# Transposes one at a time between wide products, all four of a copied tile rounded

## The chip, the cores and the metric

The kernel runs on one core of a Trainium2 chip. The metric is the device time of one execution in microseconds, median of several runs. TensorE (PE in the profile; its weight loads are PEld) multiplies, VectorE is DVE, ScalarE is ACT, GpSimd is POOL, SyncE is SP.

## The reference

A decoder trunk of 256 tokens by 2048: a latent attention layer (MLA), an MLP, a Mamba-2 layer (SSM), and a second MLP, each behind an RMS norm and added to the residual stream. All is float32.

```python
def reference(x, ...):
    for i in range(DEPTH):                       # DEPTH = 2
        h = rms_norm(x, mix_norm_g[i])
        mix = mla_mixer(h, ...) if i % 2 == 0 else ssm_mixer(h, ...)
        x = x + mix
        h = rms_norm(x, mlp_norm_g[i])
        x = x + squared_relu_mlp(h, mlp_w_in[i], mlp_w_out[i])
    return x

def squared_relu_mlp(h, w_in, w_out):            # w_in 2048 x 8192, w_out 8192 x 2048
    u = jax.nn.relu(h @ w_in)
    return (u * u) @ w_out
```

## The kernel before, in words

Every large product is done in three rounded-fp32 products (fp32r). A float32 operand is split into a high half (rounded, `wh` of a weight, `h` of an activation) and a low half (the rest, `wl`, `lo`), and high x high, low x high and high x low are added up in PSUM. The weights stream from memory once; ACT makes each high half (line 102) and VectorE each low half (line 103). A wide product has 512 columns of weights moving and a 128x128 block of activations as the stationary operand that a weight load puts in. It is issued from `block` (lines 339, 340 and 343; MLA, SSM and the end of an MLP) or from `products` in `mlp_body` (lines 616 to 618).

The stationary side must have the model dimension on the partitions, so each new activation tile of 128 tokens by 512 columns is transposed on TensorE in four 128x128 pieces into one PSUM bank (pool `sm` or `yp`) by `transposed`; ACT then copies the bank out as the high half (`split_out`, line 299) and VectorE makes the low half (line 300). For the hidden tiles of the MLP, the boundary tiles (`finalize`) and the gated tiles of the SSM layer, `words` first copies the tile with a DMA from POOL's queue into a tile of type fp32r (named `tr`), and a transpose of such a copy runs as rounded fp32 (line 322); the others run as plain fp32 (line 324). `words` takes the number of 128-column pieces that it copies. `by_words` names the hidden tiles of pairs 1 to 6 in the MLP.

TensorE's order is the order of the program's text; the orders of the other engines are set by a scheduler. Work that shall come a little later is put in a queue with `later(n, fn)` and comes out n calls of `tick` later, between two blocks. In the MLP a table of tokens made by a planner sets the order; a clock `at` counts the time that the planner gives to each token (1.36 or 2.72 us), and `turn` and `when` put transposes and other steps at due times on that clock. `combinations` makes sums of activation tiles for the seven-product scheme of the MLP; its steps `one` and `two` are due at 5 and 10 on that clock, and what they make is called `sN5`, `sN6`, `sN7`.

Whatever puts out a transposed tile, the four transposes stand in a row in TensorE's order, and where the two token tiles come in one tick, eight do. The transposes of the attention heads (`s1`, `s3`) and of the convolution (`conv`) are written out by themselves and are no part of this.

Of the kernel before, what the change touches and what calls it, by code (L numbers as in the profile page):

```python
# [28 lines left out]
P = 128  # L29
# [29 lines left out]
class Unit:  # L59
# [3 lines left out]
    def __init__(self, key, nk, n, loads, make):  # L63
        self.key, self.nk, self.n, self.loads, self.make = key, nk, n, loads, make
# [150 lines left out]
class Trunk:  # L215
    def __init__(self, tc, ctx, d, out):
        self.tc, self.nc, self.d, self.out = tc, tc.nc, d, out
        nc = self.nc
        pool = lambda name, bufs, **kw: ctx.enter_context(tc.tile_pool(name=name, bufs=bufs, **kw))
        self.c = pool("const", 1)  # L220
        self.st = pool("stat", 24)
        self.res = pool("res", 1)
        self.xtp = pool("xt", 8)
        self.k4 = pool("k4", 8)
        self.s2 = pool("s2", 7)
        self.gb = pool("gb", 2)
        self.wp = {"raw": pool("raw", 6), "wh": pool("wh", 4), "wl": pool("wl", 4)}
        self.acc = pool("acc", 4, space=PSUM)
        self.sm = pool("sm", 2, space=PSUM)
        self.yp = pool("yp", 2, space=PSUM)  # L230
        self.queue, self.pump = [], None
        self.nsm = 0
        self.uid = 0

# [19 lines left out]
    def drain(self):  # L254
        while self.queue:
            self.tick()

    def stat(self, n):
        return self.st.tile([P, 16], F32, tag="st", name=self.name("st"))[:, :n]
# [54 lines left out]
        self.transposed(src, h[:, :, sl], lo[:, :, sl], wide)  # L314

    def transposed(self, src, h, lo, wide=True):
        b = self.bank(wide)
        src, words, n = src if isinstance(src, tuple) else (src, None, 0)
        for j in range(4):
            v = slice(j * P, (j + 1) * P)  # L320
            if j < n:
                self.nc.tensor.transpose(b.bitcast(F32R)[:, v], words[:, v], self.ident_r)  # L322
            else:
                self.nc.tensor.transpose(b[:, v], src[:, v], self.ident)  # L324
        self.split_out(h, lo, b.rearrange("p (k n) -> p k n", k=4))


    def block(self, keys, lhs, n=512, accs=None, first=True, last=True, mid=None):
        nc = self.nc
        if accs is None:  # L330
            accs = [self.acc_tile() for _ in range(2)]
        kt = 0
        for ik, key in enumerate(keys):
            for nk, wh, wl, end in self.flow.piece(key):
                en = last and ik == len(keys) - 1 and end
                for q in range(nk):
                    for t in range(2):
                        ah, al = lhs(kt + q, t)
                        nc.tensor.matmul(accs[t][:, :n], ah, wh[:, q, :], start=first and kt + q == 0, stop=False)  # L339
                        nc.tensor.matmul(accs[t][:, :n], al, wh[:, q, :], start=False, stop=False)  # L340
                for q in range(nk):
                    for t in range(2):
                        nc.tensor.matmul(accs[t][:, :n], lhs(kt + q, t)[0], wl[:, q, :], start=False, stop=en and q == nk - 1)  # L343
                kt += nk
                if mid and not end:
                    mid()
            self.tick()
        return accs
# [44 lines left out]
    def finalize(self, nb, accs, wide=True):  # L393
        nc = self.nc
        g = self.gain_tile(self.nx_gain[nb])
        if not self.by_tile:
            self.nx[nb] = (self.ktile(self.xtp), self.ktile(self.xtp))
        elif nb % 2 == 0:
            for t in range(2):
                self.nx[nb // 2, t] = [self.ktile(self.xtp).rearrange("p a b -> p (a b)").rearrange("p (k n) -> p k n", n=P)  # L400
                                       for _ in range(2)]
        for t in range(2):
            if self.by_tile:
                h, lo = (v[:, 4 * (nb % 2):4 * (nb % 2) + 4] for v in self.nx[nb // 2, t])
            else:
                h, lo = (v[:, :, t * P:(t + 1) * P] for v in self.nx[nb])
            x = self.x[t][nb]
            nc.vector.tensor_tensor(x, accs[t], x, ALU.add)
            xg = self.scratch()
            nc.vector.tensor_tensor(xg, x, g, ALU.mult)  # L410
            self.square_sum(x, self.nx_ssq[:, t * 4 + nb:t * 4 + nb + 1])
            early = nb < 3 - self.by_tile
            if early:
                xg = self.words(xg, 4 - t)
            self.later(int(early), lambda h=h, lo=lo, xg=xg: self.transposed(xg, h, lo, wide))

    def boundary_end(self):
# [141 lines left out]
    def mlp_body(self, mp, layer, gain):  # L559
# [4 lines left out]
        def hidden(r, pp, j, t):  # L564

            nc.scalar.activation(r, r, AF.Square)
            if (pp, j) not in us:
                us[pp, j] = (self.ktile(self.k4), self.ktile(self.k4))
            h, lo = us[pp, j]
            if by_words(pp, j, t):  # L570
                r = self.words(r, 3, mp)
            return lambda wide: self.transposes(r, h, lo, t, wide)

        def relu(src, t):
# [10 lines left out]
        S, steps = self.combinations(mp, xa)  # L585
        S["M1"], S["N4"], S["M2"] = xa[0, 0], xa[1, 1], xa[1, 0]
        out, bank, v, count = {}, {}, {}, {}
# [3 lines left out]
        def when(us, fn):  # L591
            due.append((at[0] + us, fn))
# [16 lines left out]
        def products(accs, key, lhs, kt, first, last):  # L609
            u, (h, lo) = self.flow.next(key)  # L610
            for q in range(2):
                k = 2 * kt + q
                wh, wl = h[:, q * 512:(q + 1) * 512], lo[:, q * 512:(q + 1) * 512]
                for t, b in enumerate(accs):
                    ah, al = lhs(k, t)
                    nc.tensor.matmul(b, ah, wh, start=first and q == 0, stop=False)  # L616
                    nc.tensor.matmul(b, ah, wl, start=False, stop=False)  # L617
                    nc.tensor.matmul(b, al, wh, start=False, stop=last and q == 1)  # L618

        sub = lambda o, a, b: nc.vector.tensor_tensor(o, a, b, ALU.subtract)  # L620
        plus = lambda o, a, b: nc.vector.tensor_tensor(o, a, b, ALU.add)
# [29 lines left out]

        tokens = plan()
        inside = False
        when(5, steps[0])
        when(10, steps[1])
        for tok in tokens:
            key = (tok[0], layer) + tok[1:]
            if tok[0] == "s":
                _, p, name, d = tok
# [3 lines left out]
                if count.setdefault(name, 0) % 4 == 0:  # L663
                    pool = self.sm if name == "N7" else self.acc
                    bank[name] = pool.tile([P, 512], F32, tag=pool.name, name=self.name("st"))
                count[name] += 1
                products([bank[name]], key, lambda k, t: [x[:, k] for x in S[name]], d,
                         count[name] % 4 == 1, count[name] % 4 == 0)
                if count[name] % 4 == 0:
                    after(name, p)  # L670
                move(1.36)
            elif tok[0] == "c":
                _, p, j, o = tok
# [11 lines left out]
            else:  # L685
                _, p, nb, o = tok
# [380 lines left out]
    def ssm_body(self, sp, dp, gain):  # L1067
# [12 lines left out]
        xg = [None] * GROUPS  # L1080
# [248 lines left out]
        def z_block(g):  # L1329
            accs = self.block([("si", "z", g, q) for q in range(4)], xT)  # L1330
            ng = self.gain_tile(d["sng"][g])
            ssq = self.stat(2)
            ws = []
            for t in range(2):
                w = self.scratch()
                nc.scalar.activation(w, accs[t], AF.Tanh, scale=rsh[t])
                nc.vector.scalar_tensor_tensor(w, w, 1.0, accs[t], ALU.add, ALU.mult)
                ws.append(w)
            yT[g] = (self.ktile(self.k4), self.ktile(self.k4))

            def gate():
                if g not in ready:
                    self.later(0, gate)
                    return
                for t in range(2):
                    x = xg[g][t]
                    nc.gpsimd.tensor_tensor(x, ws[t], x, ALU.mult)
                    self.square_sum(x, ssq[:, t:t + 1], scale=rs[t])
                rr = self.rsqrt(ssq, 2, 512, 4 * EPS)
                r = self.stat(2)  # L1350
                nc.vector.tensor_tensor(r, rr, rs2, ALU.mult)
                for t in range(2):
                    nc.vector.scalar_tensor_tensor(ws[t], xg[g][t], r[:, t:t + 1], ng, ALU.mult, ALU.mult)
                    w = self.words(ws[t], 4 - t)
                    self.later(2, lambda t=t, w=w: self.transposes(w, yT[g][0], yT[g][1], t, False))
                self.later(2, lambda: gated.add(g))

            self.later(0, gate)
# [50 lines left out]
def by_words(p, j, t):  # L1409

    return 0 < p < 7
# [196 lines left out]
```

## Time and profile before

| what | value |
|---|---|
| runs | 2288.2, 2285.67, 2287.46 us; median 2287.46 us |
| profiled execution, span from first to last instruction | 2284.5 us |
| TensorE busy | 2278.1 us, 10929 products |
| VectorE, ScalarE, GpSimd busy | 84%, 61%, 12% of the span |
| TensorE clock granted | 1.000 over the span |
| rounded transposes of `transposed` (line 322) | 249 |
| plain transposes of `transposed` (line 324) | 183 |

The profile gives the span of the profiled execution, and for its own time nothing beyond it; the runs are 1.2 to 3.7 us longer than that span. Products overlap in TensorE's pipeline, so the sum of their recorded durations says little; the distance from one start to the next says what each costs. In a timeline, neighbouring instructions of one line and shape are merged into one row with a count.

### The profile page before, as it was taken

How to read it: one execution, taken by the hardware profiler on the slowest of the kernel's cores; microseconds unless marked ns; L12 is line 12 of the kernel's file. 1: busy time of each engine (PE TensorE's matmuls, PEld its weight loads, DVE VectorE, ACT ScalarE, POOL GpSimd, SP SyncE). 2: the span in 40 equal slices, each digit the busy share in tenths (PEclk: the TensorE clock that was granted, in tenths of full speed). 3: DMA queues.
4: the chain of work that ended last, by engine and by line, in shares of the span. 5: the costliest groups of instructions: out<-in, count | busy, mean ns of one | idle time of the engine just before them, and what ended most of it. 6: DMA issues, size and time to landing. Idle time of an engine off the chain costs nothing.

```text
span 2284.5 us, 30768 instructions
## 1 busy us (share of the span) xinstructions
PE 2278.1 (100%) x10929; PEld 1889.6 (83%) x10929; DVE 1915.9 (84%) x2318; ACT 1390.1 (61%) x1947; POOL 275.5 (12%) x315
## 2 busy tenths in 40 slices
PE   9999999999999999999999999999999999999999
PEld 7898888888888888888888888888888888888887
DVE  7786698999898897687899688676989889989985
ACT  7775576566666666564666555545666666666663
POOL 1440000000000000100133213121000000000000
PEclk9999999999999999999999999999999999999999
DMA  8545678888888878667888787767688888888874
GB/s 315 173 153 159 211 230 267 259 255 270 264 255 259 267 232 271 227 208 241 277 280 278 245 275 264 229 222 229 204 265 248 259 270 253 260 275 247 267 232 160
DMA packets 167706, 557.16 MB, mean 244 GB/s; under 512 B 19040, under 2 KB 28192, under 8 KB 166528
## 3 DMA queue, kind: packets, MB, share of 16 engines
q1 hardware_dynamic: 151264, 502.44, 66.2%
q0 software_dynamic: 13888, 48.49, 10.0%
q10 hardware_dynamic: 2400, 4.27, 0.5%
q8 instruction: 86, 1.41, 0.3%
q14 instruction: 68, 0.56, 0.1%
HBM read 529.65 MB, written 6.41 MB: 235 GB/s over the span
## 4 chain that ended last, share of the span: by engine, by line
PE 96%; DVE 1%; DMA 1%; ACT 1%; issue 1%; POOL 0%; SPq 0%; ACTq 0%; DVEq 0%
PE acc L339 13%; PE acc L340 13%; PE acc L343 13%; PE yp L618 9%; PE yp L617 9%; PE yp L616 9%; PE st L617 7%; PE st L618 7%; PE st L616 7%; DMA wraw<-mi 1%; PE sm L324 1%; DVE wl L103 1%; PE y L1309 1%; PE sm L322 1%; PE acc L616 1%; PE acc L618 1%
## 5 line engine op out<-in xcount | busy, mean ns | idle before, releaser
L102 ACT ACTIVATE wh<-wraw 128x1024 fp32r<-128x1024 f32 (+1 forms) x818 | 856.2, 1053 | 570.4 <-PE acc L340 268.9
L103 DVE TENSOR_TENSOR wl<-wraw,wh 128x1024 fp32r<-128x1024 f32 (+1 forms) x818 | 985.5, 1221 | 240.6 <-ACT wh L102 216.6
L616 PE MATMUL yp<-wh,k 128*128 128x512 f32 x896 | 349.2, 390 | 0.0
L618 PE MATMUL yp<-wh,k 128*128 128x512 f32 x896 | 348.8, 389 | 0.0
L617 PE MATMUL yp<-wl,k 128*128 128x512 f32 x896 | 348.6, 389 | 0.0
L339 PE MATMUL acc<-wh,xt 128*128 128x512 f32 x704 | 279.7, 397 | 0.4 <-ACT wh L102 0.4
L340 PE MATMUL acc<-wh,xt 128*128 128x512 f32 x704 | 274.9, 390 | 0.1
L102 ACT ACTIVATE wh<-wrx 128x1024 fp32r<-128x1024 f32 x168 | 177.8, 1058 | 153.4 <-PE yp L618 101.7
L103 DVE TENSOR_TENSOR wl<-wrx,wh 128x1024 fp32r<-128x1024 f32 x168 | 204.3, 1221 | 36.6 <-ACT wh L102 35.6
L618 PEld LDWEIGHTS yp<-wh,k 128*128 128x128 f32 x896 | 168.2, 188 | 35.1
L617 PEld LDWEIGHTS yp<-wl,k 128*128 128x128 f32 x896 | 168.2, 188 | 34.9
L616 PEld LDWEIGHTS yp<-wh,k 128*128 128x128 f32 x896 | 168.2, 188 | 34.8
L339 PE MATMUL acc<-wh,k 128*128 128x512 f32 x496 | 196.5, 396 | 0.0
L340 PE MATMUL acc<-wh,k 128*128 128x512 f32 x496 | 193.3, 390 | 0.0
L343 PE MATMUL acc<-wl,xt 128*128 128x512 f32 x704 | 188.3, 389 | 0.0
L616 PE MATMUL st<-wh,xt 128*128 128x512 f32 x448 | 177.7, 397 | 0.0
L618 PE MATMUL st<-wh,xt 128*128 128x512 f32 x448 | 174.9, 390 | 0.0
L617 PE MATMUL st<-wl,xt 128*128 128x512 f32 x448 | 174.7, 390 | 0.0
L339 PEld LDWEIGHTS acc<-wh,xt 128*128 128x128 f32 x704 | 132.7, 188 | 29.4 <-ACT wh L102 1.6
L340 PEld LDWEIGHTS acc<-wh,xt 128*128 128x128 f32 x704 | 132.5, 188 | 28.5 <-issue 1.2
L343 PEld LDWEIGHTS acc<-wl,xt 128*128 128x128 f32 x704 | 132.1, 188 | 27.7
L199 POOL DMA_DIRECT2D wrx<-mi x56 | 49.2, 878 | 720.6 <-DVE wl L103 524.5
(318 smaller groups left out, 3527.0 us busy)
## 6 DMA issues: line engine op xcount, KB each, us to landing
wraw<-mi SPq DMA_DIRECT2D x256, 512.0 KB, 5.5
wraw<-mo SPq DMA_DIRECT2D x256, 512.0 KB, 5.6
wraw<-si SPq DMA_DIRECT2D x160, 512.0 KB, 5.2
wraw<-so SPq DMA_DIRECT2D x64, 512.0 KB, 5.2
wrx<-mi SPq DMA_DIRECT2D x56, 512.0 KB, 5.4
wrx<-mi POOLq DMA_DIRECT2D x56, 512.0 KB, 7.8
wraw<-wo SPq DMA_DIRECT2D x32, 512.0 KB, 4.0
taps<-xD SPq DMA_DIRECT2D x16, 768.0 KB, 8.4
```

What stands on the lines that cost most here:

```text
L102: self.last = nc.scalar.activation(h[:, v], raw[:, v], AF.Copy)
L103: self.last_lo = nc.vector.tensor_tensor(lo[:, v], raw[:, v], h[:, v].bitcast(F32), ALU.subtract)
L199: nc.gpsimd.dma_start(st["b11"].tile, quarter(d, 1, 0), accum_op=ALU.add)
L322: self.nc.tensor.transpose(b.bitcast(F32R)[:, v], words[:, v], self.ident_r)
L324: self.nc.tensor.transpose(b[:, v], src[:, v], self.ident)
L339: nc.tensor.matmul(accs[t][:, :n], ah, wh[:, q, :], start=first and kt + q == 0, stop=False)
L340: nc.tensor.matmul(accs[t][:, :n], al, wh[:, q, :], start=False, stop=False)
L343: nc.tensor.matmul(accs[t][:, :n], lhs(kt + q, t)[0], wl[:, q, :], start=False, stop=en and q == nk - 1)
L616: nc.tensor.matmul(b, ah, wh, start=first and q == 0, stop=False)
L617: nc.tensor.matmul(b, ah, wl, start=False, stop=False)
L618: nc.tensor.matmul(b, al, wh, start=False, stop=last and q == 1)
L1309: nc.tensor.matmul(y[t][c, o], part(t)[:, c], xg[g][t][:, o], start=True, stop=True)
```

## The change

`transposed` no longer issues its four transposes. It puts four closures in a list `drops`, and `drip`, called behind every wide product of `block` and of `products`, issues one of them. The bank is taken with the first of the four, and the copy out of it follows the fourth. `drain` flushes what is left at the end. Where word copies are made, all four pieces of a tile are copied now and all four transposes run rounded; before it was three in the MLP's hidden tiles and in the tile of the second 128 tokens elsewhere. The two steps of the combinations are due at 8 and 12.

```diff
         self.queue, self.pump = [], None
+        self.drops = []
...
     def drain(self):
         while self.queue:
             self.tick()
+        self.flush()
+
+    def drip(self):
+        if self.drops:
+            self.drops.pop(0)()
+
+    def flush(self):
+        while self.drops:
+            self.drip()
...
     def transposed(self, src, h, lo, wide=True):
-        b = self.bank(wide)
         src, words, n = src if isinstance(src, tuple) else (src, None, 0)
-        for j in range(4):
-            v = slice(j * P, (j + 1) * P)
+        bank = []
+
+        def one(j):
+            if not bank:
+                bank.append(self.bank(wide))
+            b, v = bank[0], slice(j * P, (j + 1) * P)
             if j < n:
                 self.nc.tensor.transpose(b.bitcast(F32R)[:, v], words[:, v], self.ident_r)
             else:
                 self.nc.tensor.transpose(b[:, v], src[:, v], self.ident)
-        self.split_out(h, lo, b.rearrange("p (k n) -> p k n", k=4))
+            if j == 3:
+                self.split_out(h, lo, b.rearrange("p (k n) -> p k n", k=4))
+
+        for j in range(4):
+            self.drops.append(lambda j=j: one(j))
...
     def block(...):
                         nc.tensor.matmul(accs[t][:, :n], ah, wh[:, q, :], start=first and kt + q == 0, stop=False)
+                        self.drip()
                         nc.tensor.matmul(accs[t][:, :n], al, wh[:, q, :], start=False, stop=False)
+                        self.drip()
...
                         nc.tensor.matmul(accs[t][:, :n], lhs(kt + q, t)[0], wl[:, q, :], start=False, stop=en and q == nk - 1)
+                        self.drip()
...
     def finalize(...):
-                xg = self.words(xg, 4 - t)
+                xg = self.words(xg, 4)
...
     def hidden(...):
-                r = self.words(r, 3, mp)
+                r = self.words(r, 4, mp)
...
     def products(...):
                     nc.tensor.matmul(b, ah, wh, start=first and q == 0, stop=False)
+                    self.drip()
                     nc.tensor.matmul(b, ah, wl, start=False, stop=False)
+                    self.drip()
                     nc.tensor.matmul(b, al, wh, start=False, stop=last and q == 1)
+                    self.drip()
...
-        when(5, steps[0])
-        when(10, steps[1])
+        when(8, steps[0])
+        when(12, steps[1])
...
     def gate():
-                    w = self.words(ws[t], 4 - t)
+                    w = self.words(ws[t], 4)
```

On TensorE, in the first MLP, a hidden tile (`k`) of pair 0 is the operand of wide products while another hidden tile, copied as `tr`, is transposed into a bank of `sm`. Before:

```order
L618 MATMUL yp_3896<-wh_3866,k_433_3271 128x512
L322 MATMUL sm_3933<-ident,tr_3785 128x128 x3
L324 MATMUL sm_3933<-ident,s_457_3776 128x128
L616 MATMUL yp_3895<-wh_3878,k_445_3557 128x512
L617 MATMUL yp_3895<-wl_3879,k_445_3557 128x512
```

The three rounded transposes and the plain one stand in a row. The same place on TensorE after the change (line 335 is a rounded transpose there, 636, 638 and 640 are the wide products of `products`):

```order
L636 MATMUL yp_3895<-wh_3878,k_445_3557 128x512
L335 MATMUL sm_3940<-ident,tr_3785 128x128
L638 MATMUL yp_3895<-wl_3879,k_445_3557 128x512
L335 MATMUL sm_3940<-ident,tr_3785 128x128
L640 MATMUL yp_3895<-wh_3878,k_446_3558 128x512
L335 MATMUL sm_3940<-ident,tr_3785 128x128
L636 MATMUL yp_3896<-wh_3878,k_445_3557 128x512
L335 MATMUL sm_3940<-ident,tr_3785 128x128
L638 MATMUL yp_3896<-wl_3879,k_445_3557 128x512
```

Each transpose has a wide product on either side, the fourth is rounded too, and the row's end lies three wide products further on.

On TensorE, in the MLA stage, the two token tiles of the key and value latent (`ckv`) are transposed behind the query products of head pair 1 (384 columns) and then used. Before, eight plain transposes and the end of the query products:

```order
L324 MATMUL sm_782<-ident,s_57_706 128x128 x4
L324 MATMUL sm_789<-ident,s_58_708 128x128 x4
L339 MATMUL yp_762<-wh_728,cq_199 128x384
L340 MATMUL yp_762<-wh_728,cq_200 128x384
L339 MATMUL yp_763<-wh_728,cq_199 128x384
L340 MATMUL yp_763<-wh_728,cq_200 128x384
```

Twelve query products stood between the last transpose and the first product that reads `ckv`. After (337 is a plain transpose, 356, 358 and 362 the products of `block`):

```order
L356 MATMUL yp_763<-wh_728,cq_199 128x384
L337 MATMUL sm_800<-ident,s_58_708 128x128
L358 MATMUL yp_763<-wh_728,cq_200 128x384
L337 MATMUL sm_800<-ident,s_58_708 128x128
L362 MATMUL yp_762<-wl_729,cq_199 128x384
L362 MATMUL yp_763<-wl_729,cq_199 128x384
L362 MATMUL yp_762<-wl_729,cq_199 128x384
L362 MATMUL yp_763<-wl_729,cq_199 128x384
L356 MATMUL acc_864<-wh_746,ckv_201 128x512
L358 MATMUL acc_864<-wh_746,ckv_202 128x512
```

Four query products are left between the last transpose and the first use. On ScalarE, which waits for those transposes, before:

```order
L102 ACTIVATE wh_798<-wraw_726 128x768
L299 ACTIVATE ckv_201<-sm_782 128x4x128
L299 ACTIVATE ckv_201<-sm_789 128x4x128
L102 ACTIVATE wh_868<-wraw_744 128x768
L296 ACTIVATE s_83_828,st_827<-yp_762 128x192
```

And after, at the same place on ScalarE:

```order
L102 ACTIVATE wh_784<-wraw_726 128x768
L309 ACTIVATE ckv_201<-sm_789 128x4x128
L102 ACTIVATE wh_868<-wraw_744 128x768
L309 ACTIVATE ckv_201<-sm_800 128x4x128
L306 ACTIVATE s_83_828,st_827<-yp_762 128x192
```

A weight conversion (line 102) now stands between the two copies out of the banks.

## The prediction, made before the changed kernel was run

> **What bounds the kernel.** I read the page's busy shares and chain first, then the waits of TensorE, then the timeline around single transposes. The page:
>
> ```profile
> span 2284.5 us, 30768 instructions
> PE 2278.1 (100%) x10929; PEld 1889.6 (83%) x10929; DVE 1915.9 (84%) x2318; ACT 1390.1 (61%) x1947; POOL 275.5 (12%) x315
> PE 96%; DVE 1%; DMA 1%; ACT 1%; issue 1%; POOL 0%; SPq 0%; ACTq 0%; DVEq 0%
> ```
>
> The busy line, then the chain by engine. TensorE never stops, and the chain is TensorE to 96%. The waits of the weight loads say the same; this is the largest:
>
> ```profile
> PEld st L617 <- DVE wl L103: 3.2, 8, 0.5
> ```
>
> So 3.2 us in eight waits, of 2284. Whatever TensorE issues is paid in full: a shorter or longer place in its stream moves the end by as much, and work of the other engines counts only where it would make TensorE wait. The measure of everything is the step from one wide product to the next:
>
> ```profile
> 500.38 0.39 PE L616 MATMUL yp<-wh,k 128*128 128x512 f32 x1
> ...
> 511.26 0.39 PE L616 MATMUL st<-wh,sN 128*128 128x512 f32 x1
> ```
>
> There are 48 steps between these two, so 10.88/48 = 0.2267 us each. The recorded 0.39 is longer than the step because products overlap in the pipeline; starts are what counts.
>
> The transposes that the change touches, by shape (L322 are the rounded ones, that read a word copy; L324 the plain fp32 ones):
>
> ```profile
> L324 PE MATMUL sm<-ident,s 128*128 128x128 f32 x167 | 33.7, 281 | 0.0
> L322 PE MATMUL sm<-ident,tr 128*128 128x128 f32 x229 | 26.9, 236 | 0.0
> L324 PE MATMUL yp<-ident,s 128*128 128x128 f32 x16 | 2.4, 272 | 0.0
> L322 PE MATMUL yp<-ident,tr 128*128 128x128 f32 x20 | 2.3, 236 | 0.0
> ```
>
> 249 rounded and 183 plain, 432 in all. In the program's order they stand in 86 rows: 48 rows of three rounded and one plain, 15 of seven rounded and one plain, 16 of four plain, 7 of eight plain.
>
> **What the rows cost now.** The price of a row is the time from the last wide product before it to the second one behind it, less two steps (the second, because the first one's record starts early and is long). Three rounded and one plain:
>
> ```profile
> 374.36 0.39 PE L617 MATMUL yp<-wl,k 128*128 128x512 f32 x1
> 374.59 0.39 PE L618 MATMUL yp<-wh,k 128*128 128x512 f32 x1
> 374.82 0.37 PE L322 MATMUL sm<-ident,tr 128*128 128x128 f32 x3
> 375.02 0.30 PE L324 MATMUL sm<-ident,s 128*128 128x128 f32 x1
> ...
> 375.39 0.40 PE L617 MATMUL yp<-wl,k 128*128 128x512 f32 x1
> ...
> 377.71 0.39 PE L618 MATMUL yp<-wh,k 128*128 128x512 f32 x1
> ```
>
> 375.39 - 374.59 - 2 x 0.2267 = 0.347 us. (To 377.71 there are ten more steps, in 2.32 us and not 2.27: a tail of about 0.04 us in which wide products run a little slow, whose cause I don't know.) Seven rounded and one plain, then four plain, then eight plain:
>
> ```profile
> 231.46 0.85 PE L343 MATMUL acc<-wl,k 128*128 128x512 f32 x3
> 232.14 0.46 PE L322 MATMUL yp<-ident,tr 128*128 128x128 f32 x4
> ...
> 233.05 0.39 PE L340 MATMUL acc<-wh,k 128*128 128x512 f32 x1
> ```
>
> ```profile
> 297.85 0.39 PE L618 MATMUL yp<-wh,xt 128*128 128x512 f32 x1
> 298.08 0.60 PE L324 MATMUL sm<-ident,s 128*128 128x128 f32 x4
> ...
> 298.75 0.40 PE L617 MATMUL yp<-wl,xt 128*128 128x512 f32 x1
> ```
>
> ```profile
> 277.79 0.39 PE L618 MATMUL acc<-wh,xt 128*128 128x512 f32 x1
> 278.02 0.60 PE L324 MATMUL yp<-ident,s 128*128 128x128 f32 x4
> ...
> 279.12 0.40 PE L617 MATMUL acc<-wl,xt 128*128 128x512 f32 x1
> ```
>
> 1.59 - 4 x 0.2267 = 0.683 us (three wide products stand in the first line), 0.90 - 0.453 = 0.447 us and 1.33 - 0.453 = 0.877 us. From the pairs: one more rounded transpose in a row costs (0.683 - 0.347)/4 = 0.084 us, one more plain one (0.877 - 0.447)/4 = 0.108 us, and a row's ends add little: 0.447 - 4 x 0.108 = 0.015 us. All rows now: 48 x 0.347 + 15 x 0.683 + 16 x 0.447 + 7 x 0.877 = 16.7 + 10.2 + 7.2 + 6.1 = 40.2 us.
>
> **What they cost one by one.** Each of the 432 then stands between two wide products. Its own weight load hides behind the wide product ahead of it, as the first one's of each row does now. But the wide product behind it needs a load too, and that can start only when the transpose has taken its weights. Today one wide load in a row's four or eight is in this position; after the change all 432 are. The trace has no rounded transpose straight ahead of a wide product (each row ends with a plain one), so I bound it. Below: the columns alone, a quarter of a wide product, 0.2267/4 = 0.057 us. Above, and nearest, is the fold (L366): four products of only 64 columns, with ordinary loads, and then a wide one.
>
> ```profile
> 981.01 0.53 PEld L366 LDWEIGHTS sm<-cst,s 128*128 128x128 f32 x4
> 981.12 0.56 PE L366 MATMUL sm<-cst,s 128*128 128x64 f32 x4
> 981.46 0.19 PEld L339 LDWEIGHTS acc<-wh,xt 128*128 128x128 f32 x1
> 981.48 0.48 PE L339 MATMUL acc<-wh,xt 128*128 128x512 f32 x1
> 981.80 0.40 PE L340 MATMUL acc<-wh,xt 128*128 128x512 f32 x1
> ```
>
> 981.80 - 981.12 - 0.2267 = 0.453 us for four, 0.113 each, and the loads start 0.45/4 = 0.112 us apart. These have half the columns of a transpose, and yet cost more than its 0.084 in a row; so the ordinary load sets their step, and it takes 0.11 us where nothing wide covers it. A load that starts late says the same:
>
> ```profile
> 65.81 0.19 PEld L340 LDWEIGHTS acc<-wh,ckv 128*128 128x128 f32 x1 [0.44 <-DVE ckv L300]
> 65.35 0.40 PE L339 MATMUL acc<-wh,ckv 128*128 128x512 f32 x1
> 65.81 0.50 PE L340 MATMUL acc<-wh,ckv 128*128 128x512 f32 x1
> ```
>
> The second product, whose load waited for its operand, lasts 0.50 and not 0.40: 0.10 of uncovered load. So a lone rounded transpose costs what the wide load behind it costs, 0.113 us, and a few ns at the change from wide to narrow (374.82 - 374.59 = 0.23, not 0.227): I take 0.12. A lone plain one streams longer and covers that load, but is no cheaper: 0.108 + 0.015 = 0.12 us. Then it is the same which kind they are: 432 x 0.12 = 51.8 us.
>
> [...]
>
> **The other parts.** 63 transposes become rounded (the fourth of each such row): costed above at 0.12 like the rest, so they save nothing. Their copies grow from 192 to 256 KB:
>
> ```profile
> tr<-s POOLq DMA_DIRECT2D x63, 192.0 KB, 5.2
> tr<-s POOLq DMA_DIRECT2D x15, 256.0 KB, 4.0
> ```
>
> The large ones that there are land in 4.0 us, the smaller in 5.2, so the size is not what takes the time; and the transposes that read copies show no idle time ahead of them (0.0 in the rows of L322). I cost this at nothing, covered by the time that a copy lies ready; were that gone, each late copy would stop TensorE by its delay, in 63 places. POOL's queue, 12% busy, carries as many issues as before.
>
> The copy out of a bank follows the fourth transpose, which now comes three wide products later (0.9 us), and seven for the second group of a pair (some 2 us). How long the copy takes until both halves can be used is seen behind the row at 374.82:
>
> ```profile
> 377.25 0.68 DVE L300 TENSOR_TENSOR k<-sm,k 128x512 fp32r<-128x512 f32 x1
> ```
>
> Ready at 377.93, 2.9 us after the last transpose. Counted in the new order, the first product that needs a tile stands 3.6 us or more behind its last transpose everywhere, except for ckv in the MLA stage: 0.7 us there, where it was 2.1. That place waits already (the 0.44 above). ACT's order now has a weight conversion between its two copies, VectorE its low half: the second low half comes perhaps 0.5 us later. I add 0.5 us, from 0 to 1.5.
>
> The two steps of the combinations move from 5 and 10 to 8 and 12 on the planner's clock:
>
> ```profile
> 293.05 1.22 DVE L300 TENSOR_TENSOR sN<-xf,sN 128x1024 fp32r<-128x1024 f32 x1
> 303.02 0.48 PE L616 MATMUL st<-wh,sN 128*128 128x512 f32 x1
> ```
>
> The last of them is done at 294.3, and its kind is first read at 303.0: 8.7 us cover the 3 us. If that were gone, VectorE's conversions would be late in the first pairs of products, for a us or so in each of two MLPs.
>
> **The sum.** 51.8 - 40.2 + 0.5 = +12.1 us. Against the profiled execution's 2284.5 us that is 0.53%; the runs' median, 2287.46, lies 3 us above that span, for what lies around it. 2287.5 + 12 = 2299.5 us. What is open: the tails (86 rows by 0.04 = 3.4 us now), which may vanish or come twice as often, and the lone price, 0.11 to 0.125.
>
> **The rivals.** *Faster: the wide load hides too.* If the load for the wide product could be put in ahead of time, or its product start on a part of the load, a lone rounded transpose would cost only its columns, 0.057 us, and 312 of them 17.8 us; with 120 plain ones at 0.12, 14.4 us, and 0.5 at ckv, that is 7.5 us less than the rows: 2280 us, or 2276.5 if the tails go too. It decides at (40.2 - 0.5 - 14.4)/312 = 0.081 us for a lone rounded one. For it speaks that the in-row price, 0.084, is close to this; against it the fold's 0.113 with a wide product right behind. [...] Chance 0.18.
>
> *About the same: half hidden.* At 0.09 for a lone rounded one: 28.1 + 14.4 - 40.2 + 0.5 = +2.8 us, 2290. Chance 0.08. A measurement of this kernel can't tell less than about 0.2%, 4.6 us, from no change.
>
> *Slower still: late copies.* 14 groups have under 5 us between the last transpose and the first user; should VectorE (84% busy) run late at each and cost 0.5 us, 7 us come on top: 2306.5 us. Against it: in the rows shown 2.9 us suffice. Chance 0.06.
>
> The forecast itself has 0.68. Slower by over 0.2%: 0.68 + 0.06 = 0.74; within 0.2%: 0.08; faster: 0.18. The forecast's own range is 2291 to 2306 us (0.11 without tails to 0.125 with twice the tails and 1.5 at ckv). To leave out no more than 2 in 10 the range must reach down to the near end of the faster rival: 2282 to 2306.
>
> **What would show it.** In the timeline after, the wide products within a group of four or eight start 0.35 us apart (0.2267 + 0.12); the faster rival has 0.28 to 0.31. The wide load starts with the transpose, and the wide product behind it has a long record (0.45 or more), as at 981.48. Rounded and plain ones cost alike. Weight loads have new waits only at ckv, under 2 us in all. The prediction is wrong at its root if the wide products there are less than 0.307 us apart: then the load behind a lone transpose is not what sets its price.

## The result, and the profile after

| | before | after |
|---|---|---|
| median of four runs | 2286.82 us (2285.67 to 2288.2) | 2304.85 us (2300.6 to 2305.92) |
| ratio, 95% interval | 1 | 1.0077 [1.0063, 1.0091] |
| span of the profiled execution | 2284.5 us | 2302.9 us |

The changed kernel is slower by 18 us; 12 were forecast. The busy line of its page, the chain by engine and the row of the word copies:

```profile
PE 2290.2 (99%) x10929; PEld 1891.6 (82%) x10929; DVE 1918.6 (83%) x2318; ACT 1396.2 (61%) x1947; POOL 272.0 (12%) x315
PE 97%; DVE 1%; DMA 1%; issue 0%; ACT 0%; SPq 0%; DVEq 0%; ACTq 0%
tr<-s POOLq DMA_DIRECT2D x78, 256.0 KB, 5.5
```

TensorE is still 97% of the chain, with the same 10929 products; the other engines are busy as long as before within about one per cent. All 78 copies are large now, land in 5.5 us, and their transposes hardly wait for them. So the time is in TensorE's stream: in the transposes, or in stops. First the transposes. TensorE's timeline at one group of four, in the first MLP:

```profile
580.20 0.40 PE L636 MATMUL st<-wh,xt 128*128 128x512 f32 x1
580.43 0.22 PE L335 MATMUL sm<-ident,tr 128*128 128x128 f32 x1
580.49 0.45 PE L638 MATMUL st<-wl,xt 128*128 128x512 f32 x1
580.78 0.22 PE L335 MATMUL sm<-ident,tr 128*128 128x128 f32 x1
580.83 0.45 PE L640 MATMUL st<-wh,xt 128*128 128x512 f32 x1
```

By start plus duration the wide products end at 580.60, 580.94 and 581.28: 0.34 us apart, where 0.2267 is the step without a transpose, so about 0.115 us for each lone transpose. The ends are the profile's model; taken from start to start over each whole group, as the prediction took the rows, the median is 0.472 us for a group of four rounded ones and 0.475 for four plain ones, 0.952 and 0.946 for eight. All 432 sum to 51.9 us; counted in the same way, the rows of before sum to 40.5. The weight loads at the same place:

```profile
580.20 0.14 PEld L335 LDWEIGHTS sm<-ident,tr 128*128 128x128 f32 x1
580.44 0.19 PEld L638 LDWEIGHTS st<-wl,xt 128*128 128x128 f32 x1
```

The wide product's load starts at 580.44, 0.01 us after the start of the transpose (580.43) and not before, and lasts 0.19 us; the wide product's record starts at 580.49, while its load still runs, and is 0.45 long, not 0.40.

Then the stops. The waits of the weight loads, the two largest of those that are new or grew:

```profile
PEld yp L638 <- DVE wl L103: 6.3, 2, 3.3
PEld acc L358 <- DVE ckv L310: 2.9, 2, 1.8
```

The first are one stop at the start of each MLP: TensorE needs the low half of a weight that VectorE has not made yet. TensorE's timeline at the first of them:

```profile
296.17 0.39 PE L636 MATMUL yp<-wh,xt 128*128 128x512 f32 x1
299.13 0.50 PE L638 MATMUL yp<-wl,xt 128*128 128x512 f32 x1 [2.57 <-DVE wl L103]
299.47 0.45 PE L640 MATMUL yp<-wh,xt 128*128 128x512 f32 x1
299.72 0.63 PE L636 MATMUL yp<-wh,xt 128*128 128x512 f32 x1
300.15 0.63 PE L638 MATMUL yp<-wl,xt 128*128 128x512 f32 x1
...
303.12 0.40 PE L640 MATMUL yp<-wh,xt 128*128 128x512 f32 x1
```

From 296.17 to 299.13 one step takes 2.96 us, 2.73 too much. Then something else is seen: the next products stand 0.43 us apart, and ten steps from 299.13 to 303.12 take 3.99 us and not 2.27. The table by stretches, whose third figure from the right is the granted clock, shows why, in the stretch in which the clock was down:

```profile
299.68:303.09 3.41, 3.41 (x9) 2.65 (x8) 3.41 (x4) 0.18 (x1) 0.00 (x0) 0.50 0.86 304
```

From 299.68 on the granted clock was 0.50 for 3.41 us. With that the stop costs 2.73 + 1.72 = 4.45 us; the one in the second MLP, read in the same way (1641.39 to 1644.66, then ten steps to 1648.58), 3.04 + 1.65 = 4.69.

The other place is ckv in the MLA stage, in TensorE's timeline:

```profile
64.99 0.39 PE L356 MATMUL acc<-wh,ckv 128*128 128x512 f32 x1
66.10 0.50 PE L358 MATMUL acc<-wh,ckv 128*128 128x512 f32 x1 [0.72 <-DVE ckv L310]
...
68.20 0.50 PE L358 MATMUL acc<-wh,ckv 128*128 128x512 f32 x1 [1.37 <-DVE ckv L310]
68.54 0.39 PE L356 MATMUL acc<-wh,ckv 128*128 128x512 f32 x1
```

Four steps in 3.55 us, 2.64 more than 4 x 0.2267; before, the same four (from 65.35 to 66.74) were 0.48 over. So +2.2 us.

The account of the two profiled executions: transposes 51.9 - 40.5 = +11.4, the two stops +9.1, ckv +2.2. Against that, small waits of before are gone (those of line 617 on `wl`, 3.2 us by the wait table, are 0.6 us in two now): 1.8 us there by TensorE's steps, 1.2 us at two places of the MLA stage, some 0.7 in the tails. The sum is +19.0 us; the spans differ by 18.4, and the 0.6 between them is left open.

### The profile page after: what moved, and what is told of

It is laid out like the page before. It is cut to its first block, busy times and chain, and to the rows that moved or that the text cites. A ratio compares the mean times of both kernels' runs of the same rounds, so it can differ in the third digit from the quotient of the medians.

```text
span 2302.9 us, 30769 instructions
## 1 busy us (share of the span) xinstructions
PE 2290.2 (99%) x10929; PEld 1891.6 (82%) x10929; DVE 1918.6 (83%) x2318; ACT 1396.2 (61%) x1947; POOL 272.0 (12%) x315
## 4 chain that ended last, share of the span: by engine, by line
PE 97%; DVE 1%; DMA 1%; issue 0%; ACT 0%; SPq 0%; DVEq 0%; ACTq 0%
PE acc L356 13%; PE acc L358 13%; PE acc L362 13%; PE yp L638 9%; PE yp L636 9%; PE yp L640 9%; PE st L638 8%; PE st L636 8%; PE st L640 8%; DMA wraw<-mi 1%; PE sm L335 1%; PE y L1332 1%; PE acc L748 0%; DVE wl L103 0%; PE sm L337 0%; PE sm L378 0%
```

## The experiments

Two things were in dispute; each ratio below is to the kernel before. *What a lone transpose costs:* by the load theory, the uncovered load of the wide product behind it, whatever its width; by the rival, its own columns and a fixed cost on top. *What makes the stops at the start of the MLPs:* theory A, the combinations' steps, due at 8 and 12 and no longer at 5 and 10; theory B, that the transposes of the boundary tile come one by one, so that VectorE gets the second tile later and does its work in another order.

### The stops: due times back, and the boundary tile in rows

The eight transposes that are still in the list when an MLP starts are put out in a row, and the due times go back:

```diff
-        when(8, steps[0])
-        when(12, steps[1])
+        when(5, steps[0])
+        when(10, steps[1])
...
                     self.tick()
+                    if at[0] < 5:
+                        self.flush()
```

> The changed kernel with the due times of the combinations' two steps back at 5 and 10; so that they can be, the eight transposes of the last boundary tile at the start of each MLP are issued in a row again, all others one by one. Theory A (the later due times push ten VectorE operations into a stretch where they hold up a weight's low half): the stops of 2.7 and 3.0 us at the start of the two MLPs, with the slow products behind them about 4.5 us each, go; 2305 - 9 = 2296 us. Rival (the transposes one by one are late and that alone makes the stops): the two rows of eight take part of it away as well, so this run tells less against it than the next; if neither matters, 2305 us. Lone transposes elsewhere keep their step of 0.345 us from wide to wide product under both.

2297.69 us, ratio 1.0049 [1.0034, 1.0064], span 2295.9. No wait on `wl` is left at the start of the MLPs. So without the stops the median is 7 us lower, and one of the two edits, or both, took them away.

### The due times alone, in the kernel before

```diff
-        when(5, steps[0])
-        when(10, steps[1])
+        when(8, steps[0])
+        when(12, steps[1])
```

> The kernel before, rows as they were, with only the two due times moved to 8 and 12. Theory A (due times make the stops at the start of the MLPs): two new waits of a product for a weight's low half there, of 2 to 3 us, with slow products behind them: 2287 + 9 = 2296 us. Rival (late transposes make them): no new wait, 2287 us, within 2.

2286.58 us, ratio 1.0 [0.999, 1.0009]. VectorE's timeline, at the two conversions for which the changed kernel stops:

```profile
293.38 2.36 DVE L103 TENSOR_TENSOR wl<-wraw,wh 128x1024 fp32r<-128x1024 f32 x2
```

They come no later than in the kernel before (294.18, below), and TensorE has no new wait. With rows the later due times cost nothing: theory A falls, in so far as it speaks of the due times alone.

### Four behind one wide product, and two

`drip` puts out four of the list at a time, or two (`range(2)` in the second kernel); all else is as in the changed kernel, with due times at 8 and 12.

```diff
     def drip(self):
-        if self.drops:
-            self.drops.pop(0)()
+        for _ in range(4):
+            if self.drops:
+                self.drops.pop(0)()
```

> The changed kernel with all of it kept (the list, the due times, four rounded transposes), but each drop issues four transposes in a row behind one wide product. Load theory (the wide product behind the last transpose of a row pays an uncovered weight load of about 0.118 us, the others 0.084): rows of four rounded cost 0.35 and of four plain 0.447 us, 78 x 0.35 + 30 x 0.447 = 40.7 us against 51.9 one by one; so 11 us less than the changed kernel, 2294 us, with the stops at the start of the MLPs still there. The fourth rounded one gains nothing over a plain one: 0.35 as before. Rival (a place's price is that of the switch from wide to narrow columns, whatever is loaded): a row of four rounded costs 4 x 0.067 + 0.05 = 0.32 us, 2292 us.

> The changed kernel with two transposes behind each wide product. Load theory: a pair of rounded ones costs 0.118 + 0.084 = 0.202 us, a pair of plain ones 0.119 + 0.109 = 0.228: 156 x 0.202 + 60 x 0.228 = 45.2 us, 6.7 us less than one by one: 2298 us, the stops at the start of the MLPs included. If lone transposes were dear for their lateness or for the order of the other engines and not for the load, the pair costs twice a lone one, 0.236, and the time stays at 2305 us.

Fours: 2287.82 us, ratio 1.0006 [0.9997, 1.0016]. Pairs: 2290.42 us, ratio 1.0017 [1.0008, 1.0027]. TensorE's timeline, a row of four rounded ones:

```profile
375.29 0.39 PE L637 MATMUL yp<-wh,k 128*128 128x512 f32 x1
375.52 0.46 PE L336 MATMUL sm<-ident,tr 128*128 128x128 f32 x4
...
376.12 0.40 PE L641 MATMUL yp<-wh,k 128*128 128x512 f32 x1
```

376.12 - 375.29 - 2 x 0.2267 = 0.377 us (median of all such rows 0.370), that is three in-row transposes at 0.084 and one at 0.118. And two pairs:

```profile
374.88 0.39 PE L637 MATMUL yp<-wh,k 128*128 128x512 f32 x1
375.11 0.28 PE L336 MATMUL sm<-ident,tr 128*128 128x128 f32 x2
...
375.95 0.39 PE L637 MATMUL yp<-wh,k 128*128 128x512 f32 x1
```

1.07 - 3 x 0.2267 = 0.39 us for both, 0.195 each (the median by pair is 0.2025, for plain ones 0.23): one at 0.084 and one at 0.118. All transposes sum to 43.0 us with fours, 45.7 with pairs and 51.9 one by one. The more rows the transposes are split into, the more wide products have an uncovered load, and behind rounded ones each such load adds some 0.034 us (0.118 - 0.084), as the load theory has it.

Both have the late due times, and neither stops at the start of the MLPs. VectorE's timeline with pairs:

```profile
294.05 2.36 DVE L103 TENSOR_TENSOR wl<-wraw,wh 128x1024 fp32r<-128x1024 f32 x2
297.45 1.23 DVE L183 TENSOR_TENSOR wraw<-wraw,wraw 128x1024 f32<-128x1024 f32 x1
```

The conversions come at 294.05, ahead of the addition of line 183. That speaks against A a second time. Both kernels came out 6 to 8 us below what was expected: the transposes cost a little more than expected (43.0 us and not 40.7 with fours, 45.7 and not 45.2 with pairs), but the expectations had kept the stops.

### Late due times, only the boundary tile in a row

The same as the first experiment, without its change of the due times:

```diff
                     self.tick()
+                    if at[0] < 5:
+                        self.flush()
```

> The changed kernel, due times at 8 and 12 as changed, with one thing undone: the eight transposes of the last boundary tile at the start of each MLP are issued in a row. Theory B (these eight come up to 2.3 us later when they stand one by one, and the scheduler then sets an addition of the next product, which waits for its DMA, ahead of VectorE's sums; the two due times have no part in it): the two stops at the start of the MLPs go, with the slow products behind them, 2 x 4.4 us: 2305 - 9 = 2296 us, as in the run with the due times back. Rival (due times and late transposes are both needed for the stops to go): the stops stay, 2304 us.

2297.47 us, ratio 1.0047 [1.003, 1.0064]; no stop at the start of the MLPs. It is as fast as the first experiment, so the due times add nothing, and the row of eight is what removes the stops: theory B. (The reverse, one by one with due times at 5 and 10, was not tried.)

### How lateness becomes a stop: one addition moved

VectorE's timeline in the changed kernel, from the first sum of the second boundary tile (line 548) to the two conversions:

```profile
285.06 1.22 DVE L548 TENSOR_TENSOR xf<-xt,xt 128x1024 f32<-128x1024 f32 x1
287.63 1.23 DVE L183 TENSOR_TENSOR wraw<-wraw,wraw 128x1024 f32<-128x1024 f32 x1 [1.36 <-DMA wraw<-mi]
288.78 1.22 DVE L558 TENSOR_TENSOR xf<-xf,xf 128x1024 f32<-128x1024 f32 x1
...
297.86 2.35 DVE L103 TENSOR_TENSOR wl<-wraw,wh 128x1024 fp32r<-128x1024 f32 x2
```

And in the kernel before:

```profile
294.18 2.35 DVE L103 TENSOR_TENSOR wl<-wraw,wh 128x1024 fp32r<-128x1024 f32 x2
...
297.59 1.22 DVE L183 TENSOR_TENSOR wraw<-wraw,wraw 128x1024 f32<-128x1024 f32 x1
```

Line 183 adds two weights for the seven-product scheme. Before, its first addition stands behind the conversions. With the second boundary tile late, VectorE's order has it ahead of the sums of line 558, at 287.63: there it waits 1.36 us for a weight's DMA and takes 1.15 us itself, and all behind it comes that much later. In the next experiment only this first addition of each MLP is held in VectorE's order (by `HOLD(flow)`) behind the low half that was made last before it in the program, and the boundary tile comes one by one again:

```diff
-                add("b22", "b12", "b22")
+                with HOLD(flow) if (p, d) == (1, 0) else nullcontext():
+                    add("b22", "b12", "b22")
```

> As the run before it, but only the first addition for a product N7 in each MLP is held (the one that the changed kernel's VectorE order has ahead of the sums); the others stand as the scheduler sets them, so that the waits of the run before in the later pairs should be gone. Theory B: the stops at the start of both MLPs shrink to 0.3 us, the slow products behind them go, nothing else changes: 2305 - 8 = 2297 us. Rival (holding it back only moves the wait to the next pair, as in the run before): 2303 us or more.

2298.37 us, ratio 1.005 [1.0033, 1.0067]. Its waits on `wl`:

```profile
PEld yp L647 <- DVE wl L110: 1.1, 2, 0.5
```

6.3 us in two waits have become 1.1. Elsewhere the rows of the wait table differ by less than 1 us from those of the changed kernel; the largest such difference is 0.9, in TensorE's waits for ACT's `wh`. TensorE's timeline at the first of them:

```profile
298.44 0.39 PE L645 MATMUL yp<-wh,xt 128*128 128x512 f32 x1
298.94 0.50 PE L647 MATMUL yp<-wl,xt 128*128 128x512 f32 x1
299.28 0.40 PE L649 MATMUL yp<-wh,xt 128*128 128x512 f32 x1
299.51 0.40 PE L645 MATMUL yp<-wh,xt 128*128 128x512 f32 x1
```

The step that was 2.96 us is 0.50, and no slow stretch follows. So most of the stop is the addition's new place, and what remains, some 0.3 us by that step, is the lateness itself.

A cruder version holds every addition of that kind:

```diff
-                add("b22", "b12", "b22")
+                with HOLD(flow):
+                    add("b22", "b12", "b22")
```

> The changed kernel with all transposes one by one and the due times as changed; only the addition for each product N7 is held in VectorE's order until the low half made last before it in the program has been issued, as it stood in the order before. Theory B: the addition took 1.15 us and 1.36 us of waiting for its DMA out of VectorE's time just ahead of the sums; without it the weight's low half comes some 2.5 us sooner, the stops of 2.7 and 3.0 us shrink to 0.2 to 0.5, too short for the slow products behind them: 2305 - 8 = 2297 us. Rival (the late copies of the last boundary tile alone make the stops): 2.5 of the 2.7 us stay, 2304 us.

2309.88 us, ratio 1.0103 [1.0088, 1.0118]: slower than the changed kernel itself. The wait table:

```profile
PEld st L647 <- DVE wl L110: 11.7, 18, 1.5
```

The stop at the start shrank as in the other version, but with the other additions held there are 18 waits of 11.7 us in all, where the changed kernel has two of 0.6. The 2297 us that were expected were missed, and as a test of theory B by its time this kernel says nothing; it shows only that holding all of these additions costs more than it saves.

### The price: all plain, and products of four widths

All 432 run as plain fp32, still one by one; the word copies are made and not read.

```diff
-            if j < n:
-                self.nc.tensor.transpose(b.bitcast(F32R)[:, v], words[:, v], self.ident_r)
-            else:
+            if True:
                 self.nc.tensor.transpose(b[:, v], src[:, v], self.ident)
```

> The changed kernel with all 432 transposes plain fp32, one by one (the word copies are still made, but nothing reads them on TensorE). Load theory: a lone plain one streams twice, 0.107 us and a little, just as long as the wide load behind it needs, so it costs the 0.119 us of a lone rounded one; 2305 us, within 2. Rival (the columns set the price, or a fixed switch beside them): 312 transposes cost 0.05 us more each, 2320 us.

2324.67 us, ratio 1.0173 [1.0156, 1.019]: 20 us more than was expected. The price is as expected, a median of 0.477 us for a group of four, 0.119 each. No run shows the two streams of 0.107 us that the expectation takes for a plain one; by the records plain ones in a row start 0.109 us apart in the kernel before, and a lone one lasts 0.27 us in the changed kernel. The rest is in waits; the largest row:

```profile
PEld yp L636 <- DVE wl L103: 22.8, 13, 3.2
```

VectorE's timeline and TensorE's, at one of these 13:

```profile
479.64 1.23 DVE L183 TENSOR_TENSOR wraw<-wraw,wraw 128x1024 f32<-128x1024 f32 x1 [1.80 <-DMA wraw<-mi]
480.78 2.35 DVE L103 TENSOR_TENSOR wl<-wraw,wh 128x1024 fp32r<-128x1024 f32 x2
```

```profile
480.15 0.39 PE L634 MATMUL yp<-wh,k 128*128 128x512 f32 x1
482.05 0.50 PE L636 MATMUL yp<-wl,k 128*128 128x512 f32 x1 [1.51 <-DVE wl L103]
```

It is the pattern of the stops again, an addition that waits for its weight in front of the conversions, now inside the MLPs. That a plain transpose instead of a rounded one changes VectorE's order there was not expected; which of the order's rules does it I did not find out.

The second kernel measures the price by itself. Ahead of the four transposes of each copied tile in the MLPs it issues four extra rounded products of 64, 128, 256 and 384 columns, each alone between two wide products; their results are overwritten. `probing` is set in the MLPs alone.

```diff
+        def probe(c):
+            if not bank:
+                bank.append(self.bank(wide))
+            self.nc.tensor.matmul(bank[0][:, :c], words[:, :P], words[:, :c], start=True, stop=True)
+
+        if self.probing and n == 4:
+            for c in (64, 128, 256, 384):
+                self.drops.append(lambda c=c: probe(c))
```

> A measurement of the price by itself: the changed kernel with four more lone products ahead of the four transposes of each copied tile in the MLPs, ordinary rounded products of the copy with itself that write 64, 128, 256 and 384 columns into the bank that the transposes then overwrite, each behind a wide product. What counts is the step from the wide product ahead to the wide product behind, less 0.2267 us. Load theory (the load behind the narrow product is uncovered as long as the narrow product is short): 0.118 us for 64, for 128 and about 0.12 for 256, and 0.173 for 384, its own columns. Rival (own columns and a fixed price for the switch, which the lone transposes put at 0.05): 0.09, 0.118, 0.17 and 0.224 us.

One run, 2347.59 us, with stops that the other kernels don't have, so only the prices count. TensorE's timeline, the last three of a group:

```profile
582.62 0.48 PE L649 MATMUL st<-wl,sN 128*128 128x512 f32 x1
582.93 0.22 PE L345 MATMUL sm<-tr 128*128 128x128 f32 x1
582.99 0.45 PE L651 MATMUL st<-wh,sN 128*128 128x512 f32 x1
583.28 0.28 PE L345 MATMUL sm<-tr 128*128 128x256 f32 x1
583.40 0.39 PE L647 MATMUL st<-wh,sN 128*128 128x512 f32 x1
583.63 0.33 PE L345 MATMUL sm<-tr 128*128 128x384 f32 x1
583.80 0.39 PE L649 MATMUL st<-wl,sN 128*128 128x512 f32 x1
```

The wide products end (start plus duration) at 583.10, 583.44, 583.79 and 584.19: 0.34, 0.35 and 0.40 apart, so 0.11, 0.12 and 0.17 us for 128, 256 and 384 columns. The medians over 54 of each are 0.115, 0.116, 0.121 and 0.183 for the four widths. From 64 to 256 columns the price stays within 6 ns while the columns grow fourfold; only 384 columns, whose own 0.17 us (384/512 of a wide step) are longer than the load's 0.12, cost about their own time. Of the rival's numbers, 0.09 to 0.224, none but that for 128 columns is near. The load theory holds for these widths: a narrow product between two wide ones cost the larger of its columns (0.183 us for 384) and the load behind it (0.115 to 0.121 for 64 to 256).

Of the two ways in which the faster rival has the load hidden, the records show this. The load of the transpose (580.20) starts with the wide product ahead of it, but that of the wide product behind it (580.44) was not put in ahead of the transpose's start (580.43). The wide product (580.49) does start before its load, 0.19 us long, is through, but it saves nothing here, since the products' ends are 0.34 us apart.

## Why the prediction was right in its sign and short in its size

- **The price of a lone transpose: right.** Taken 0.12 us from the fold's rows, measured 0.118 to 0.119, rounded and plain alike. The term was +11.6 us and came to +11.4.
- **The faster rivals fall.** The wide products stand 0.34 us apart by their ends and not 0.28 to 0.31; the load behind the transpose isn't hidden, not even by half. This is shown by the trace and by the four widths.
- **Copies of 256 KB at nothing: right.** The waits of the rounded transposes are 1.2 us in three, all for VectorE's `k` and none for a copy. The copies land in 5.5 us, and not in the 4.0 of the fifteen large ones of before, so the prediction read the size too favourably; but nothing waited for them.
- **ckv: the right place and too small.** Taken +0.5 us (0 to 1.5), measured +2.2. What was estimated is that the second low half comes 0.5 us later than the first; the first also came late, and the two waits add up. The sign that was named, new waits only at ckv and under 2 us in all, failed at both places.
- **The start of the MLPs: the step that failed.** "8.7 us cover the 3 us" was about the combinations' due times, and for these it was right: moved alone they cost nothing. But the rule for late tiles, that the first *product* which needs a tile must stand far enough behind its last transpose, looked at TensorE alone. The boundary tile's first user is a sum on VectorE, and its lateness changed VectorE's order: an addition that waits 1.36 us for its weight got in front of two conversions. "A us or so in each of two MLPs", the price named if the cover went, was 4.45 and 4.69 us, since the stops themselves were 2.73 and 3.04 us and the half clock behind them (0.50 for 3.41 us each) cost 1.72 and 1.65.
- **The late-copies rival** (7 us on top, in 14 places) had the size but not the mechanism: one place in each MLP, not all, and not the copy itself.
- **The sum.** +12.1 was forecast and +18.4 measured in the spans: +9.1 for the stops, +1.7 more at ckv, -0.2 on the transposes, and -3.7 for waits and tails that went away, which the prediction had not counted as a gain; 0.6 stays open. That the time still lies in the forecast's own range of 2291 to 2306 us is partly luck: its upper end was made of a dearer transpose, twice the tails and 1.5 us at ckv. The first two did not come, and the stops, which the range had at nothing, took their place.

None of the kernels tried is faster than before. Rows are the cheapest form, the best of them (fours) can't be told from the kernel before, and a plain transpose at a row's end is no loss: 0.353 us is the median of three rounded and one plain, 0.370 of four rounded.

## What to carry to other kernels

Where TensorE is the bound, keep narrow products together: here one more rounded transpose in a row cost 0.084 us and a lone one 0.118, since only the wide product behind a row paid a load that nothing covered; split into more pieces, the same transposes cost 43.0 us in fours, 45.7 in pairs and 51.9 one by one. If something is made later, follow it to its first user on every engine, and ask what a scheduler puts in the gap: an instruction that waits for a DMA may get in front of what TensorE needs (1.36 us of waiting here). Price a stop of TensorE above the wait itself: here 2.73 and 3.04 us came to 4.45 and 4.69 with the half clock behind them.

## What was not expected of the hardware

**Behind some stops the granted clock was 0.50 for 3.41 us.** In the changed kernel's trace this came twice inside the work, from 299.68 and from 1644.53, each time near the end of the stop at the start of an MLP (299.13 and 1644.66); in the 3.41 us ahead TensorE was busy for 0.84 and 0.66 us. At ckv the changed kernel has waits of 0.72 and 1.37 us, and the kernel with only the boundary tile in a row 0.72 and 1.38, but only the second had half clock there. Stretches of that length around the waits, first in the changed kernel, then in the other (stretch, length, TensorE's busy time; third from the right the granted clock):

```profile
64.16:67.57 3.41, 1.95 (x10) 1.12 (x8) 3.41 (x10) 2.57 (x10) 0.81 (x1) 1.00 0.63 210
67.57:70.98 3.41, 2.78 (x12) 2.32 (x13) 0.58 (x1) 1.06 (x1) 3.25 (x6) 1.00 0.59 175
```

```profile
66.29:69.70 3.41, 1.38 (x5) 0.85 (x6) 2.71 (x7) 1.51 (x9) 2.09 (x3) 1.00 0.58 167
69.70:73.11 3.41, 3.41 (x10) 2.66 (x9) 1.20 (x6) 1.06 (x1) 2.02 (x4) 0.50 0.39 142
```

In the other kernel TensorE is busy for 1.38 us of the first stretch, and the next has half the clock. In the changed kernel it is busy for 1.95 and 2.78 us, and the clock stays at 1.00. But a stretch of the same length that is laid over both waits there (65.38 to 68.79) holds only 1.32 us, and behind it, from 68.79 to 72.20, the clock is 1.00 too. So nearly the same stop brought the half clock in one execution and not in the other; what decides it is not shown.

The spread of the changed kernel's runs would fit. The one of 2300.6 us had a mean granted clock of 1.000, the other three, of 2304.69 to 2305.92 us, 0.999 or 0.998, and the two stretches of half clock in the profiled one cost 1.72 + 1.65 = 3.4 us. Only one of the four has a profile here, so this is not shown.

**A plain transpose was the cheaper one at the end of a row.** Alone it had the longer record (0.27 us, and 0.22 for a rounded one) and cost the same (0.119 and 0.118 us); behind three rounded ones it was 17 ns cheaper than a fourth rounded one (0.353 and 0.370 us for the row). Why is not shown.
